# Latent attention: a tile of keys meets all 512 queries of a head in one product with the values, and the last 16 queries join the same products

## The chip, the cores and the metric

One Trainium2 chip, one of its cores. The metric is the device time of one execution of the whole program, in microseconds (us), the median of several runs. Five engines work side by side: PE (TensorE, matrix products; PEld is its loading of stationary operands), DVE (VectorE), ACT (ScalarE), POOL (GpSimd) and SP, which issues the DMAs. PE writes its results to PSUM, eight banks of 128 x 512 f32 numbers.

## What is computed

The reference is a stack of layers over 512 tokens of width 1024. Two layers of gated convolution and retention come first, then a state-space mixer with a feed-forward network, then a layer of latent attention with a second feed-forward network. Sixteen meta tokens are put ahead of the sequence for the second half, so that attention sees 528 positions. The change touches the attention alone:

```python
blocks = [(0, N_META)] + [(s, min(s + ATTN_BLOCK, L)) for s in range(N_META, L, ATTN_BLOCK)]
for s, e in blocks:
    sc = jnp.einsum('bqhd,bkhd->bhqk', q[:, s:e], k[:, :e]).astype(jnp.float32) * scale
    mask = jnp.arange(e)[None, :] <= jnp.arange(s, e)[:, None]
    p = jax.nn.softmax(jnp.where(mask, sc, -jnp.inf), axis=-1).astype(v.dtype)
    outs.append(jnp.einsum('bhqk,bkhd->bqhd', p, v[:, :e]))
```

There are 16 heads with values of width 64. The attention is causal, so a query meets only the keys up to its own position. The result needs only the 512 queries behind the meta tokens.

## The kernel before, in words

The program is written with a scheduling layer: the code names instructions and tiles, and a scheduler sets the order of the instructions on each engine, by their dependencies and the buffers that are free. A tile pool hands out buffers by tag; a tile whose tag has n buffers waits until the tile n before it has been read for the last time.

The attention runs over four groups of four heads (`b`). `project(b)` (line 1262) makes the group's keys `K`, values `v` and queries `Q` from latent rows with products of lines 382 and 397; `attend(b)` (line 1372) follows, and the scheduler mixes the projection of group b + 1 into the attention of group b. In the last group, products of the output projection (line 382, tiles `mh_a`, `ml_a`) are mixed in instead.

Inside `attend` the last 16 queries are taken first, for all four heads at once (`S`, lines 1377 to 1392): their probabilities, transposed, stand in `pt4`. Then come two pairs of heads (`hp`), and in each pair four blocks of queries (`i` = 0 to 3; 112 queries in block 0, else 128). Block i of a head meets keys 0 to 128(i + 1):

- scores: one product into a bank of three (`S`, line 1404), and one that adds the causal mask (line 1405);
- softmax (line 1353): DVE takes the maximum and scales it (1357, 1360), ACT the exponential (1363), DVE the reciprocal and the scaling (1367, 1369);
- transposes: PE turns the probabilities 128 keys at a time into one of two banks (`main2`, `main3`, line 1410), and ACT copies the bank to the tile `pT` (line 1411), of which there are three buffers;
- values: for each tile `c` of 128 keys and each head `e` of the pair one product of 64 columns of values with 112 or 128 columns of `pT` (line 1417). Head e = 0 fills partitions 0 to 63 of bank 7 (`side3`), e = 1 partitions 64 to 127.

After block 3 the last 16 queries follow, five tiles of keys for each head, products of 16 columns (line 1422). Then ACT casts the bank to `mh_a` and DVE makes the rest `ml_a` (`split`, lines 416 to 419). So a pair has 20 products of line 1417 and 10 of line 1422, and the stage has 8 pairs. An f32 product of the program shows as two instructions in the trace.

```python
for c in range(i + 1):
    for e in range(2):
        h = 2 * hp + e
        nc.tensor.matmul(op[64 * e : 64 * e + 64, q0 : q0 + M], v[:, c, 64 * h : 64 * h + 64],
                         pts[e][:, c, :M], start=(c == 0), stop=(c == i))
```

Of the kernel before, what the change touches and what calls it, by code (L numbers as in the profile page):

```python
# [9 lines left out]
F32 = mybir.dt.float32  # L10
# [7 lines left out]
P = 128  # L18
D = 1024
SEQ = 512  # L20
META = 16
T2 = SEQ + META
# [96 lines left out]
def build(ctx, tc, a):  # L119
    nc = tc.nc  # L120
# [94 lines left out]
    BANK = [PB[i // 2][:, i % 2] for i in range(4)] + side  # L215
# [195 lines left out]
    def mix_tile(name):  # L411
        h = ring.tile([P, T2], F32R, tag="mixh", name=f"mh_{name}", bufs=NRING)
        l = ring.tile([P, T2], F32R, tag="mixl", name=f"ml_{name}", bufs=NRING)
        return h, l
# [36 lines left out]
    with ExitStack() as c1:  # L451
        bp = c1.enter_context(tc.tile_pool(name="bp", bufs=1))

        def tmp(name, bufs=7):
            return bp.tile([P, 512], F32, tag="tmp", name=name, bufs=bufs)
# [164 lines left out]
        for l in range(2):  # L620

            mixc = []
            for p in range(4):
# [23 lines left out]
                for n, ps in dense((l, "z", p), X):  # L647
# [4 lines left out]
                    m = mix_tile(f"c{l}{p}{n}")  # L652
# [34 lines left out]
            for p in range(4):  # L687
# [12 lines left out]
                v = bp.tile([P, 4, 256], F32, tag="v", name=f"v{l}{p}", bufs=2)  # L700
# [14 lines left out]
                for n in range(2):  # L715
                    h = 2 * p + n
# [20 lines left out]
                    op = (D0, D1)[n]  # L737
# [12 lines left out]
                for n in range(2):  # L750
                    h = 2 * p + n
                    V.tensor_scalar(ss[:, 8 + 4 * n : 12 + 4 * n], ss[:, 8 + 4 * n : 12 + 4 * n],
                                    rc[:, 24 + h : 25 + h], None, ALU.mult)
                for n in range(2):
                    h = 2 * p + n
                    op = (D0, D1)[n]
# [8 lines left out]
                    m = mix_tile(f"r{l}{h}")  # L765
# [72 lines left out]
    with ExitStack() as c2:  # L838
# [91 lines left out]
        for g in range(8):  # L930
# [37 lines left out]
            for c, (t0, W) in enumerate(CH):  # L968
                ts_ = slice(t0, t0 + W)
                nm = f"{g}_{c}"  # L970
# [13 lines left out]
                M = sp.tile([P, 4, P], F32, tag="M", name=f"M{nm}", bufs=2)  # L984
# [12 lines left out]
                for n in range(2):  # L997
                    for cross in range(2 if c > 0 else 1):
                        for i in range(2):
                            h = 2 * n + i  # L1000
# [29 lines left out]
            if g < 7:  # L1030
# [5 lines left out]
                for i in range(4):  # L1036
                    nc.tensor.matmul(D1[32 * i : 32 * i + 32, :132], e1, sq[0][:, 132 * i : 132 * i + 132],
                                     start=True, stop=True)
# [23 lines left out]
            for n in range(2):  # L1062
                V.scalar_tensor_tensor(gz[n], gz[n], gcol(V_SNG, 2 * g + n), rb, ALU.mult, ALU.mult)
                m = mix_tile(f"s{g}{n}")
# [89 lines left out]
    with c4:  # L1154
        ap = c4.enter_context(tc.tile_pool(name="ap", bufs=1))
# [11 lines left out]
                mw[0] = ws.next(("mi", t // 2))  # L1167
            return dense2(mw[0], t % 2, X, 8)

        lsm = [tmp(f"lsm{i}", "lsm", 2) for i in range(2)]  # L1170
        lat = []
        for t in range(5):
            ps = mdense(t)
# [8 lines left out]
            else:  # L1182
                v = tmp(f"lsq{t}")
# [19 lines left out]
        def bank(kind):  # L1203
            c = cyc[kind]
            c[0] += 1
            return c[1][(c[0] - 1) % len(c[1])]
# [146 lines left out]
        def softmax(nm, S, r_, st):  # L1353

            M = S[0][0].shape[0]
            for j, (sp_, _, _) in enumerate(S):
                V.tensor_reduce(st[:M, j : j + 1], sp_, mybir.AxisListType.X, ALU.max, negate=True)
            if len(S) == 2:
                V.tensor_tensor(st[:M, 0:1], st[:M, 0:1], st[:M, 1:2], ALU.min)
            V.tensor_tensor(st[:M, 0:1], st[:M, 0:1], r_, ALU.mult)  # L1360
            p = ap.tile([P, T2], F32, tag="p", name=f"p{nm}", bufs=3)
            for j, (sp_, c0, c1_) in enumerate(S):
                nc.scalar.activation(p[:M, c0:c1_], sp_, AF.Exp, bias=st[:M, 0:1], scale=r_,
                                     accum_out=st[:M, 4 + j : 5 + j])
            if len(S) == 2:
                V.tensor_tensor(st[:M, 4:5], st[:M, 4:5], st[:M, 5:6], ALU.add)
            V.reciprocal(st[:M, 2:3], st[:M, 4:5])
            L = S[-1][2]
            V.tensor_scalar(p[:M, :L], p[:M, :L], st[:M, 2:3], None, ALU.mult)
            return p  # L1370

        def attend(b, Qh, Kh, v, rq):
            def stats(nm):
                return ap.tile([P, 8], F32, tag="st", name=f"st{nm}", bufs=4)


            S = [(bank("S")[:, :HW], HW * j, HW * j + HW) for j in range(2)]
            for j, (sp_, c0, c1_) in enumerate(S):
                for h in range(4):
                    o = sp_[32 * h : 32 * h + 32]  # L1380
                    nc.tensor.matmul(o, Qh[:, h, SEQ - 32 : SEQ], Kh[:, h, c0:c1_], start=True, stop=(j == 0))
                    if j == 1:
                        nc.tensor.matmul(o[:, HW - META :], idb[:, :32], mneg[:, META : 2 * META], start=False, stop=True)
            p = softmax(f"{b}t", S, rq[:, 16:17], stats(f"{b}t"))
            pt4 = ap.tile([P, 5, P], F32, tag="pT4", name=f"pT4{b}", bufs=1)
            pst = bank("pt")
            for c in range(4):
                nc.tensor.transpose(pst[:, P * c : P * c + P], p[:, P * c : P * c + P], ident)
            nc.scalar.copy(pt4[:, :4], pst.rearrange("p (c q) -> p c q", c=4))
            ps0 = bank("pt")[:, :P]  # L1390
            nc.tensor.transpose(ps0, p[:, T2 - P : T2], ident)
            nc.scalar.copy(pt4[:, 4], ps0)
            for hp in range(2):
                op = BANK[7]
                for i in range(4):
                    L = P * (i + 1)
                    q0 = max(0, P * i - META)
                    M = P * (i + 1) - META - q0
                    pts = []
                    for e in range(2):  # L1400
                        h = 2 * hp + e
                        nm = f"{b}{h}{i}"
                        sp_ = bank("S")[:M, :L]
                        nc.tensor.matmul(sp_, Qh[:, h, q0 : q0 + M], Kh[:, h, :L], start=True, stop=False)  # L1404
                        nc.tensor.matmul(sp_[:, L - P :], idb[:, P - M :], mneg, start=False, stop=True)
                        p = softmax(nm, [(sp_, 0, L)], rq[:M, 4 * i + h : 4 * i + h + 1], stats(nm))
                        pt = ap.tile([P, 4, P], F32, tag="pT", name=f"pT{nm}", bufs=3)
                        pst = bank("pt").rearrange("p (c q) -> p c q", c=4)
                        for c in range(i + 1):
                            nc.tensor.transpose(pst[:, c, :M], p[:M, P * c : P * c + P], ident[:M, :M])  # L1410
                        nc.scalar.copy(pt[:, : i + 1, :M], pst[:, : i + 1, :M])
                        pts.append(pt)

                    for c in range(i + 1):
                        for e in range(2):
                            h = 2 * hp + e
                            nc.tensor.matmul(op[64 * e : 64 * e + 64, q0 : q0 + M], v[:, c, 64 * h : 64 * h + 64],  # L1417
                                             pts[e][:, c, :M], start=(c == 0), stop=(c == i))
                for c in range(5):
                    for e in range(2):  # L1420
                        h = 2 * hp + e
                        nc.tensor.matmul(op[64 * e : 64 * e + 64, SEQ - META :], v[:, c, 64 * h : 64 * h + 64],
                                         pt4[:, c, 32 * h + META : 32 * h + 32], start=(c == 0), stop=(c == 4))
                m = mix_tile(f"a{b}{hp}")
                split(m, op, slice(0, SEQ))
                mix.append(m)
# [139 lines left out]
```

## Time and profile before

| | before |
|---|---|
| median of the runs (lowest to highest) | 2527.95 us (2523.36 to 2529.31), 3 runs |
| the profiled execution: its time, its span | 2524.17 us, 2522.4 us |
| instructions in the span | 41020 |
| PE, PEld, DVE, ACT, POOL busy | 98%, 87%, 64%, 43%, 6% |
| granted TensorE clock | 0.992 of full speed |
| attention stage | about 1958 to 2137 us of the span |

The profile is of one execution. Between its span and its time lie 1.8 us of start and end. Busy time of an engine is the union of its instructions; a product's shown end is a model, so two products that follow each other overlap in the rows, and the time that one really takes of PE is the distance from its start to the next one's start. "Idle before" is the time in which an engine had nothing in flight, with what ended it. Line numbers in rows are those of the kernel before.

### The profile page before, as it was taken

What the parts mean: (1) busy time and instruction counts of PE and PEld (TensorE: products, weight loads), DVE (VectorE), ACT (ScalarE), POOL (GpSimd) and SP (SyncE); (2) the same over time, 40 slices, a digit from 0 to 9 for tenths busy, and PEclk for the clock granted to TensorE, in tenths of its full rate; (3) what the DMA queues carried; (4) which work ended last, traced back from release to release, by engine and by line L of the source; (5) the groups of instructions that cost most, each with busy time, mean ns of one, the idle gap of its engine ahead of it and who ended that gap; (6) DMA issues with size and microseconds to landing.
All of it is one profiled execution on the core that took longest, in us unless ns stands there. A gap on an engine that the chain in (4) does not pass through costs nothing.

```text
span 2522.4 us, 41020 instructions
## 1 busy us (share of the span) xinstructions
PE 2460.4 (98%) x16991; PEld 2201.8 (87%) x16991; DVE 1620.4 (64%) x2968; ACT 1076.3 (43%) x2030; POOL 151.6 (6%) x177
## 2 busy tenths in 40 slices
PE   8999999989999999889999999999999999999999
PEld 7888888878888888789999998999998666999999
DVE  6743555464425554877848889777765666967764
ACT  4422332333223334455525546344344665644432
POOL 1000000100000001022202200000011000000000
PEclk9999999999999999999999999999999999999999
DMA  4333222223232222233323332233221120232322
GB/s 147 105 100 97 80 84 80 71 84 91 93 109 68 84 84 67 70 91 95 101 89 100 88 87 84 87 101 101 84 95 58 51 72 33 90 106 97 109 86 84
DMA packets 220490, 220.93 MB, mean 88 GB/s; under 512 B 8972, under 2 KB 212877, under 8 KB 220304
## 3 DMA queue, kind: packets, MB, share of 16 engines
q1 hardware_dynamic: 215648, 207.50, 26.6%
q0 software_dynamic: 4176, 10.69, 1.8%
q8 instruction: 133, 2.18, 0.3%
q14 instruction: 53, 0.43, 0.1%
q10 hardware_dynamic: 480, 0.13, 0.0%
HBM read 215.47 MB, written 2.83 MB: 87 GB/s over the span
## 4 chain that ended last, share of the span: by engine, by line
PE 84%; DVE 9%; ACT 3%; issue 2%; DMA 1%; POOL 1%; ACTq 0%; SPq 0%; DVEq 0%; POOLq 0%
PE pb L382 44%; PE main L397 7%; PE side L334 6%; PE pb L397 4%; PE main L382 3%; PE main L334 3%; PE pb L334 3%; PE pb L390 2%; PE side L1404 1%; PE side L1417 1%; DVE wlo L75 1%; PE side L1003 1%; PE side L1012 1%; PE main L1410 1%; ACT whi L74 1%
## 5 line engine op out<-in xcount | busy, mean ns | idle before, releaser
L74 ACT CAST whi<-wraw 128x1024 fp32r<-128x1024 f32 (+2 forms) x301 | 302.7, 1045 | 615.8 <-PE pb L382 430.6
L75 DVE TENSOR_TENSOR wlo<-wraw,whi 128x1024 fp32r<-128x1024 f32 (+2 forms) x301 | 364.4, 1233 | 122.5 <-ACT whi L74 120.2
L382 PE MATMUL pb<-xl_n,whi 128*128 128x264 f32 (+1 forms) x1136 | 318.1, 330 | 0.0
L382 PE MATMUL pb<-xh_n,whi 128*128 128x264 f32 (+1 forms) x1136 | 317.8, 329 | 0.3 <-DVE zu L958 0.3
L382 PE MATMUL pb<-xh_n,wlo 128*128 128x264 f32 (+1 forms) x1136 | 315.6, 329 | 0.0
L382 PEld LDWEIGHTS pb<-xh_n,whi 128*128 128x128 f32 x1136 | 192.9, 190 | 20.1 <-issue 1.2
L382 PEld LDWEIGHTS pb<-xl_n,whi 128*128 128x128 f32 x1136 | 191.9, 189 | 19.7 <-issue 1.7
L382 PEld LDWEIGHTS pb<-xh_n,wlo 128*128 128x128 f32 x1136 | 192.1, 190 | 17.6 <-issue 0.2
L382 PE MATMUL pb<-xl_l,whi 128*128 128x512 f32 x416 | 164.9, 396 | 0.0
L382 PE MATMUL pb<-xh_l,wlo 128*128 128x512 f32 x416 | 164.9, 396 | 0.0
L382 PE MATMUL pb<-xh_l,whi 128*128 128x512 f32 x416 | 164.5, 395 | 0.0
L397 PE MATMUL main<-whi,mh_w 128*128 128x256 f32 x512 | 143.8, 281 | 0.3
L397 PE MATMUL main<-whi,ml_w 128*128 128x256 f32 x512 | 143.2, 281 | 0.0
L397 PE MATMUL main<-wlo,mh_w 128*128 128x256 f32 x512 | 143.2, 281 | 0.0
L103 ACT CAST whi<-wraw 128x1024 fp32r<-128x1024 f32 x64 | 65.7, 1046 | 139.3 <-issue 54.4
L90 ACT CAST wsh<-wsr 128x512 fp32r<-128x512 f32 x96 | 58.7, 618 | 106.9 <-DVE wsr L96 62.3
L382 PE MATMUL pb<-ml_u,whi 128*128 128x264 f32 x512 | 104.2, 285 | 0.2
L382 PE MATMUL pb<-mh_u,whi 128*128 128x264 f32 x512 | 103.8, 284 | 0.0
L382 PE MATMUL pb<-mh_u,wlo 128*128 128x264 f32 x512 | 103.6, 284 | 0.0
L397 PEld LDWEIGHTS main<-whi,mh_w 128*128 128x128 f32 x512 | 96.6, 189 | 1.1 <-ACT mh_w L418 0.9
L397 PEld LDWEIGHTS main<-whi,ml_w 128*128 128x128 f32 x512 | 96.7, 189 | 0.0
L397 PEld LDWEIGHTS main<-wlo,mh_w 128*128 128x128 f32 x512 | 96.1, 188 | 0.0
(688 smaller groups left out, 6556.2 us busy)
## 6 DMA issues: line engine op xcount, KB each, us to landing
wraw<-w_in SPq DMA_DIRECT2D x63, 1024.0 KB, 5.9
wraw<-mlp_w_up SPq DMA_DIRECT2D x32, 1024.0 KB, 5.5
wraw<-mlp_w_down SPq DMA_DIRECT2D x32, 1024.0 KB, 5.3
wraw<-w_out SPq DMA_DIRECT2D x16, 1024.0 KB, 5.2
wraw<-ssd_w_in SPq DMA_DIRECT2D x16, 1024.0 KB
wraw<-ssd_w_in SPq DMA_DIRECT2D x16, 512.0 KB, 5.4
ab<-acsD POOLq DMA_DIRECT2D x32, 256.0 KB, 3.8
kR<-ke SPq DMA_DIRECT2D x32, 132.0 KB, 3.0
```

Source lines behind the costliest of these rows:

```text
L74: nc.scalar.copy(hv[s], rv[s])
L75: eng.tensor_tensor(lv[s], rv[s], hv[s].bitcast(F32), ALU.subtract)
L90: nc.scalar.copy(h, sr[:, n])
L103: nc.scalar.copy(hi[:, c], raw[:, c])
L334: nc.tensor.matmul(ps, w[wq][a][:, k], X(xq, b, k), start=(k == 0 and wq + xq == 0), stop=(k == 3 and wq == 1))
L382: nc.tensor.matmul(ps, w[wq][:, k, wsl], x(xq, k, cs), start=(k == 0 and wq + xq == 0), stop=(k == nk - 1 and wq == 1))
L390: nc.tensor.matmul(ps, w[wq][:, k, wsl], x(xq, k, cs), start=(k == 0 and wq + xq == 0), stop=(k == nk - 1 and wq == 1))
L397: nc.tensor.matmul(ps, x(xq, k, ts_), w[wq][:, k, csl], start=(k == 0 and wq + xq == 0), stop=(k == nk - 1 and xq == 1))
L1003: nc.tensor.matmul(o, xd[:W, h], M[:W, h, :W], start=True, stop=(c == 0))
L1012: nc.tensor.matmul(st[:, :256], Bt[:W], xw[:W].rearrange("p h e -> p (h e)"), start=True, stop=True)
L1404: nc.tensor.matmul(sp_, Qh[:, h, q0 : q0 + M], Kh[:, h, :L], start=True, stop=False)
L1410: nc.tensor.transpose(pst[:, c, :M], p[:M, P * c : P * c + P], ident[:M, :M])
```

## The change

For each pair of heads, `pT` becomes one tile per head, of four tiles of keys by all 512 queries. The blocks of queries are taken in the order 3, 2, 1, 0, and ACT copies each block's transposed probabilities to its columns of that tile. Beside block 3's copy one more copy takes the last 16 queries of the head out of `pt4` (first four tiles of keys) into the tile's last 16 columns. Only when all four blocks are copied come the value products: for tile `c` of keys and each head one product with all queries that see it, 512, 400, 272 and 144 columns, and one of 16 columns for the fifth tile of keys. A pair has 10 products in place of 30, with 1344 columns a head before and after. The first one is kept at its place in the program's order by `keep_in_program_order`. The tag `pT` has two buffers, four times as large, in place of three, and the two tiles `lsm` of the stage's start use one of them ahead of time.

```diff
-        lsm = [tmp(f"lsm{i}", "lsm", 2) for i in range(2)]
+        lsm = ap.tile([P, 4, SEQ], F32, tag="pT", name="lsm", bufs=2).rearrange("p c q -> p (c q)")
+        lsm = [lsm[:, T2 * i : T2 * i + T2] for i in range(2)]
...
             for hp in range(2):
-                op = BANK[7]
-                for i in range(4):
+                pts = [ap.tile([P, 4, SEQ], F32, tag="pT", name=f"pT{b}{hp}{e}", bufs=2) for e in range(2)]
+                for i in (3, 2, 1, 0):
...
-                        pt = ap.tile([P, 4, P], F32, tag="pT", name=f"pT{nm}", bufs=3)
...
-                        nc.scalar.copy(pt[:, : i + 1, :M], pst[:, : i + 1, :M])
-                        pts.append(pt)
-
-                    for c in range(i + 1):
-                        for e in range(2):
-                            h = 2 * hp + e
-                            nc.tensor.matmul(op[64 * e : 64 * e + 64, q0 : q0 + M], v[:, c, 64 * h : 64 * h + 64],
-                                             pts[e][:, c, :M], start=(c == 0), stop=(c == i))
+                        nc.scalar.copy(pts[e][:, : i + 1, q0 : q0 + M], pst[:, : i + 1, :M])
+                        if i == 3:
+                            nc.scalar.copy(pts[e][:, :, SEQ - META :], pt4[:, :4, 32 * h + META : 32 * h + 32])
+
+                op = BANK[7]
                 for c in range(5):
+                    q0 = max(0, P * c - META)
                     for e in range(2):
                         h = 2 * hp + e
-                        nc.tensor.matmul(op[64 * e : 64 * e + 64, SEQ - META :], v[:, c, 64 * h : 64 * h + 64],
-                                         pt4[:, c, 32 * h + META : 32 * h + 32], start=(c == 0), stop=(c == 4))
+                        pt = pts[e][:, c, q0:] if c < 4 else pt4[:, 4, 32 * h + META : 32 * h + 32]
+                        m = nc.tensor.matmul(op[64 * e : 64 * e + 64, q0:], v[:, c, 64 * h : 64 * h + 64], pt,
+                                             start=(c == 0), stop=(c == 4))
+                        if c + e == 0:
+                            tc.keep_in_program_order(m)
```

The scheduler builds a new order of the stage from this. In the order of PE before, the products of lines 1417 and 1422 stand in 52 groups with other work between them; here PE in group 1, first pair, block 2 (`pT102`, `pT112`: group 1, heads 0 and 1, block 2; `side3` is the bank of the values):

```order
L1404 MATMUL side2_72<-K1_17669,Q1_17668 112x128
L1405 LDWEIGHTS idb_12627
L1405 MATMUL side2_72<-mneg_12626,idb_12627 112x128
L1417 MATMUL side3_73<-pT102_18432,v1_17765 64x128
L382 MATMUL main0_17370<-ml_lat1_17115,whi154_18205 128x512
L1417 MATMUL side3_73<-pT112_18446,v1_17765 64x128
L1417 MATMUL side3_73<-pT102_18432,v1_17765 64x128
L1417 MATMUL side3_73<-pT112_18446,v1_17765 64x128
L1417 MATMUL side3_73<-pT102_18432,v1_17765 64x128
L1417 MATMUL side3_73<-pT112_18446,v1_17765 64x128
L1410 MATMUL main2_17372<-ident_79,p103_18462 128x128 x4
```

The change, PE at the end of the same pair (there the transposes are line 1409, the value products line 1420; `p110` is block 0 of head 1, `p123` block 3 of the next pair's first head):

```order
L382 MATMUL main1_17370<-mh_lat0_17060,wlo154_18157 128x512
L1409 MATMUL main3_17372<-ident_79,p110_18416 128x112
L1420 MATMUL side3_73<-pT100_18318,v1_17764 64x512
L1420 MATMUL side3_73<-pT101_18319,v1_17764 64x512
L1420 MATMUL side3_73<-pT100_18318,v1_17764 64x400
L1420 MATMUL side3_73<-pT101_18319,v1_17764 64x400
L1420 MATMUL side3_73<-pT100_18318,v1_17764 64x272
L1420 MATMUL side3_73<-pT101_18319,v1_17764 64x272
L1420 MATMUL side3_73<-pT100_18318,v1_17764 64x144
L1420 MATMUL side3_73<-pT101_18319,v1_17764 64x144
L1420 MATMUL side3_73<-pT41_18310,v1_17764 64x16 x2
L1409 MATMUL main2_17371<-ident_79,p123_18443 128x128 x4
```

All value products of the pair stand together, directly behind the last transpose of the pair. In six of the eight pairs they stand in one group so. In the first pair of group 0 and the second of group 2 the first product stands apart; PE in the first of these:

```order
L1409 MATMUL main3_17372<-ident_79,p010_17929 128x112
L1420 MATMUL side3_73<-pT000_17831,v0_17544 64x512
L1404 MATMUL side1_71<-K0_17448,Q0_17447 128x384
L1420 MATMUL side3_73<-pT001_17832,v0_17544 64x512
L1420 MATMUL side3_73<-pT000_17831,v0_17544 64x400
L1420 MATMUL side3_73<-pT001_17832,v0_17544 64x400
L1420 MATMUL side3_73<-pT000_17831,v0_17544 64x272
```

A score product of the next pair stands between head 0's first product and head 1's. On ACT, the end of group 1's first pair in the change (exponentials are line 1364, copies line 1410):

```order
L1364 ACTIVATE p110_18416,st110_18413<-side0_70,st110_18413,rq1_18136 112x128
L1410 COPY pT100_18318<-main2_17371 128x112
L1364 ACTIVATE p123_18443,st123_18440<-side1_71,st123_18440,rq1_18136 128x512
L1410 COPY pT101_18319<-main3_17372 128x112
L1364 ACTIVATE p133_18458,st133_18455<-side2_72,st133_18455,rq1_18136 128x512
L1364 ACTIVATE p122_18473,st122_18470<-side0_70,st122_18470,rq1_18136 128x384
L1322 ACTIVATE qs20_18572<-main0_17369 128x512
L418 CAST mh_a10_18432<-side3_73 128x512
L1410 COPY pT110_18436<-main2_17371 128x4x128
```

Between the last two copies that the value products wait for stands an exponential of the next pair; the cast of the bank and the next pair's first copy, which both wait for the value products, stand three instructions behind.

## Rows read from the trace of the kernel before

**Rows 1.** The chain that ended last, 1958 to 2137 us, by engine and line.

```profile
by line: PE main L382 21.0%; PE side L1404 20.1%; PE side L1417 16.0%; PE main L1410 11.0%; PE main L397 5.4%; PE side L1381 3.8%; PE side L1422 3.0%; PE main L1325 2.6%; ACT K L1274 2.6%; PE side L1405 2.4%; issue 1.8%; DVE p L1369 1.4%; A
```

**Rows 2.** Engines' busy time in the stage and in one stretch between pairs.

```profile
core 0: us, PE busy (x) PEld busy (x) DVE busy (x) ACT busy (x) POOL busy (x), PEclk, DMA share, GB/s
1958.00:2137.00 179.00, 173.21 (x1260) 118.34 (x1259) 115.31 (x417) 113.35 (x292) 7.97 (x5) 1.00 0.17 53
2004.10:2029.10 25.00, 24.71 (x202) 17.66 (x199) 15.81 (x71) 19.07 (x54) 0.00 (x0) 1.00 0.14 41
```

**Rows 3.** PE's timeline, group 1, first pair: start, length, line, out<-in, count, idle before.

```profile
2015.66 0.41 PE L1417 MATMUL side<-pT,v 128*64 128x112 f32 x2
2016.00 0.32 PE L1410 MATMUL main<-ident,p 112*128 112x112 f32 x1
...
2017.23 0.41 PE L1417 MATMUL side<-pT,v 128*64 128x112 f32 x2
2017.57 0.23 PE L1405 MATMUL side<-mneg,idb 128*128 128x128 bf16 x1
...
2019.28 1.02 PE L1404 MATMUL side<-K,Q 128*128 128x512 f32 x2
2020.23 0.66 PE L1417 MATMUL side<-pT,v 128*64 128x128 f32 x8
2020.82 0.55 PE L1410 MATMUL main<-ident,p 128*128 128x128 f32 x3
...
2022.56 0.43 PE L1417 MATMUL side<-pT,v 128*64 128x128 f32 x2
2022.92 0.50 PE L382 MATMUL main<-ml_lat,whi 128*128 128x512 f32 x1
2023.35 0.87 PE L1417 MATMUL side<-pT,v 128*64 128x128 f32 x10
2024.15 0.66 PE L1410 MATMUL main<-ident,p 128*128 128x128 f32 x4
...
2026.39 0.43 PE L1417 MATMUL side<-pT,v 128*64 128x128 f32 x2
2026.75 0.31 PE L1410 MATMUL main<-ident,p 112*128 112x112 f32 x1
...
2027.75 0.98 PE L1417 MATMUL side<-pT,v 128*64 128x128 f32 x13
...
2029.31 0.54 PE L1410 MATMUL main<-ident,p 112*128 112x112 f32 x3
```

**Rows 4.** PE's timeline, a window that holds the second of two instructions alone.

```profile
2019.71 0.59 PE L1404 MATMUL side<-K,Q 128*128 128x512 f32 x1
```

**Rows 5.** PE's timeline, the first and the last visit of the stage.

```profile
1978.83 0.41 PE L1417 MATMUL side<-pT,v 128*64 128x112 f32 x2
...
2134.79 0.98 PE L1417 MATMUL side<-pT,v 128*64 128x128 f32 x13
```

**Rows 6.** Groups of ACT in the stage by shape: count, busy us, mean ns, idle before.

```profile
L1411 ACT COPY pT<-main 128x112 f32<-128x112 f32 x16 | 3.8, 261 | 0.8 <-PE main L1410 0.7
L418 ACT CAST mh_a<-side 128x512 fp32r<-128x512 f32 x8 | 4.7, 586 | 9.1 <-PE side L1422 9.1
L1363 ACT ACTIVATE p<-side,st,rq 112x128 f32<-112x128 f32 x16 | 7.3, 457 | 0.4 <-DVE st L1360 0.4
```

**Rows 7.** ACT's timeline, the copy behind the four transposes at 2024.15.

```profile
2024.90 0.58 ACT L1411 COPY pT<-main 128x512 f32<-128x512 f32 x1 [0.68 <-PE main L1410]
```

**Rows 8.** Timeline of PE and ACT around the longest wait of a value product.

```profile
2037.05 0.40 PE L382 MATMUL main<-mh_lat,wlo 128*128 128x512 f32 x1
...
2038.48 0.47 ACT L1411 COPY pT<-main 128x384 f32<-128x384 f32 x1
...
2039.00 0.43 PE L1417 MATMUL side<-pT,v 128*64 128x128 f32 x2 [1.55 <-ACT pT L1411]
```

**Rows 9.** Waits of the stage: who waited for whom, us in total, times, longest.

```profile
PEld side L1417 <- ACT pT L1411: 10.6, 22, 2.0
```

More of the change, by code (lines that the diff above doesn't have):

```diff
@@ L1398, in attend @@
                     M = P * (i + 1) - META - q0
-                    pts = []
                     for e in range(2):
```

## The prediction

> **What bounds the kernel now.** I read the chain of waits first, for the stage that the change touches. It is nearly all PE: scores, transposes, value products (line 1417, 16.0%) and last queries (line 1422, 3.0%) stand in it beside the projections, and ACT and DVE hold a few per cent [rows 1]. The windows say the same: in the 179 us of the stage PE has something in flight for 173.2, while DVE has 115.3 and ACT 113.4, and the granted clock is 1.00, the upper level of 2.4 GHz [rows 2]. So what PE no longer has to do shortens the stage, unless ACT or DVE then fail to follow.
>
> The third view is PE's timeline over one pair of heads. Here the reader should look at distances between starts. The value products come in seven visits: 2 instructions, 2, 8, 2, 10, 2 and 34 (13 in the row, one more and the 20 of line 1422 behind it) [rows 3]. Between two score instructions of 512 columns lie 0.43 us (2019.28 to 2019.71) [rows 3, 4]; the next should start at 2020.14, and the value products start at 2020.23: **0.09 us to enter**. By the same pace an instruction of 128 columns takes 0.43 x 128 / 512 = 0.107. The eight of that visit take 0.59 until the next work starts, which fits four steps of 0.107 (two heads side by side on their halves of the array) and **0.16 to start and leave**. A visit of two instructions of one head takes 0.34 to 0.36: two steps with the other half empty, and the same overhead.
>
> **The value products before and after.** From entry to next work the seven visits take 0.34 + 0.34 + 0.59 + 0.36 + 0.80 + 0.36 + 1.56 = 4.35 us [rows 3], with 7 x 0.09 ahead of them 4.98. The order of PE has 52 visits in the stage, the first and the last at 1978.8 and 2134.8 [rows 5], 6.5 a pair, so this pair stands for the eight: 8 x 4.98 = 39.8. As a check, 19.0% of 179 us are 34.0 on the chain [rows 1], which counts the time to enter with the work before.
>
> After the change a pair is one visit. Each head streams 512 + 400 + 272 + 144 = 1328 columns in two instructions a product, both heads side by side: 2 x 1328 x 0.43 / 512 = 2.23. A step of 16 columns is what the last visit leaves: 1.56 less 0.16 less 7 x 0.107 is 0.65 for ten steps, 0.065 each [rows 3]; two remain, 0.13. With 0.09 and 0.16 that is **2.61**. The number of columns is the same; what goes is six entries and exits, the steps with one half empty, and eight of ten steps of 16 columns. Saved: 8 x (4.98 - 2.61) = 19.0.
>
> Two pairs are split: head 0's first product, 2 x 0.43 = 0.86, runs with the other half empty, and there is a further visit of 0.25. That gives back 2 x 1.1 = 2.2. **PE has 16.8 us less to do.**
>
> **What is added.** ACT gets 16 copies of 64 columns. No row has that shape; the nearest, 112 columns, takes 0.261 [rows 6]. With nothing and 0.261 as ends I take the upper: 4.2 us on ACT, hidden, since ACT would be at 117.6 of some 165 us. Uncovered they would be 4.2 us of the end.
>
> The value products now wait for the pair's last copy. From the last transpose's start this is 0.31 (the row at 2026.75), 0.09 until ACT starts (2024.15 + 0.66 to 2024.90), 0.26 of copy and 0.05 until PE starts (2038.48 + 0.47 to 2039.00), in all 0.71 [rows 3, 6, 7, 8]. The transpose's own 0.10 and the 0.09 to enter lie inside, so about 0.5 stands open where nothing lies between. By the new order three pairs are so placed (group 0's second, group 1's first, group 3's second), group 3's first has one projection product between, the others have enough. That is 1.8; ACT may also run an exponential of the next pair between the last two copies, for which I add 1.2. Today a value product's weights wait for such a copy 22 times, 10.6 in all, 0.48 each [rows 9]: eight of those would be 3.9. The ends are 0 and 8 x 1.55 = 12.4, the longest wait of today in every pair [rows 8]. I take **3**, near the mean.
>
> Behind those waiting products on PE stand the next pair's transposes; for them wait ACT's cast of the bank (0.59) and, since `pT` has two buffers, the next pair's first copy. On ACT three instructions of other work stand ahead of that cast, and on PE two sets of transposes and scores follow the products, so I cost this at nothing; without that cover it is the slower case below. The blocks' new order moves long softmaxes to the pair's start and the shortest to its end: no cost. DVE's work is the same, in another order. On SP one load of the query weights goes behind the broadcasts of a group's last head and one load of the output weights goes ahead of others; both are needed only in later work: nothing. The memory of `lsm` is free long before the first `pT`: nothing.
>
> **Sum.** 2524.17 - 16.8 + 3 = **2510.4** against the profiled execution, which stands 3.8 below the median of the runs, near their lower end. A median of new runs should lie at this or a few us above; I say 2511. With the ends of the open terms: 2504 if waits are hidden and some of today's go, 2520 if each pair waits 1.55.
>
> **The rivals.**
>
> *ACT sets the pace where the next group is projected.* In the stretch between the pairs of two groups (2004.1 to 2029.1) ACT is busy 19.07 of 25.0 us [rows 2]. With two copies more and 2.4 us less it would be 19.6 of 22.6, 87%, in a queue that runs in order. If such stretches stay as long as now, three of eight pairs give back 2.4 each: 7 us, **2517**. Against it: elsewhere in the stage ACT has a third of its time free.
>
> *PE does not bind.* In this stage weights load for only 118.3 of 179 us [rows 2], and PE waits 1.55 us for ACT at one value product [rows 8]. If the softmaxes' path through DVE and ACT sets the pace, PE's saving turns into waits: **2524**. The Trainium skill, Perfetto Trace Analysis, "Identifying the Most-Contended Engine", holds that matmul busy time is no good measure of how near PE is to its limit and that the share of weight loading is. By that rule a third of the stage would be headroom and this case likely. The distances between starts speak against it: 0.43 after 0.43 after 0.09, with no gap for a wait.
>
> *The halves do not run side by side over 512 columns.* Then a visit takes 2.3 us longer, and nothing is won: **2527** with the waits. The eight instructions in 0.59 us speak against it.
>
> *Slower: the pair becomes a closed loop.* All value products wait for the last softmax, and all copies of the next pair wait for the last value product. If the scheduler's cover is too thin, PE stands through exponential (0.46), reciprocal and scaling on DVE (taken as long), transpose, gaps and copy (0.71) before the products, and through cast and first copy (0.59 + 0.58) behind them: 2.8 [rows 6, 7]. With the exponential of the next pair in between, 3.3 a pair: 8 x 3.3 - 16.8 = 9.6 over today, **2534**. It decides from 16.8 / 8 = 2.1 of new wait a pair. For it: today's cast already waits 9.1 us in 8 times for PE [rows 6]. Against it: the order puts scores and projections of later work between.
>
> **How the numbers follow.** About 0.3%, 7.6 us, is what a measurement of this kernel can tell from no change. The forecast, 2503 to 2516, gets 0.72; ACT 0.13, half of it faster by more than 0.3%; PE not binding 0.06; halves 0.03; slower 0.06. So faster 0.77, same 0.17, slower 0.06. The range takes in the forecast's bounds and the ACT case: 2502 to 2521.
>
> **What would show it.** In the new profile the stage should be some 14 us shorter, with 10 visits of value products of about 2.6 us, each with starts of the two heads close together and steps near 0.43, 0.33, 0.23 and 0.12; the group of value products should fall from 480 instructions to 160. Waits of PE for `pT` copies should come to 3 us, not 12. ACT near 118 busy. If visits take 5 us, the halves did not overlap; if they are 2.6 and the stage is not shorter, PE's idle time will name ACT or DVE; and time that moves outside the stage would mean that the projections were only shifted.

## The result, and the profile after

| | before | after |
|---|---|---|
| median of the runs (lowest to highest) | 2526.24 us (2523.36 to 2529.31), 4 runs | 2512.99 us (2510.87 to 2515.09), 4 runs |
| the profiled execution: its time, its span | 2524.17 us, 2522.4 us | 2515.09 us, 2513.2 us |
| granted TensorE clock of that execution | 0.992 | 0.991 |

The changed kernel is faster: the ratio is 0.9947, 95% interval 0.9934 to 0.9961, which is 10 to 17 us. Forecast were 2511 us and 2502 to 2521. The two profiled executions differ by less than the medians, 9.2 us of span, since that of before lies below its median and that of after is the slowest of its four.

The windows first, with the columns of [rows 2]: the stage, which is now shorter, and the stretch from the end of group 0's last value visit to the end of group 1's first, which was 2004.28 to 2029.31 before.

```profile
core 0: us, PE busy (x) PEld busy (x) DVE busy (x) ACT busy (x) POOL busy (x), PEclk, DMA share, GB/s
1958.00:2128.50 170.50, 163.43 (x951) 107.73 (x950) 115.88 (x418) 114.71 (x310) 8.08 (x5) 1.00 0.18 55
2008.79:2031.87 23.08, 22.80 (x140) 16.18 (x139) 15.11 (x61) 18.48 (x50) 0.00 (x0) 1.00 0.17 45
```

PE's busy time falls from 173.2 to 163.4, and the stage shortens by nearly the same amount; DVE and ACT do what they did, ACT 1.4 us more. The chain that ended last, over the same stretch, answers to [rows 1]:

```profile
by line: PE main L382 20.7%; PE side L1404 18.4%; PE side L1420 13.9%; PE main L1409 10.8%; PE main L397 6.2%; PE side L1382 4.1%; PE main L1326 2.7%; ACT K L1275 2.6%; DVE p L1370 2.5%; DMA kR<-ke 2.4%; PE side L1405 1.8%; issue 1.8%; PE m
```

Lines have moved by one or three: 1420 is the value product, 1409 the transpose, 1410 ACT's copy. The value products fell from 19.0% of 179 us to 13.9% of 170.5, and more of the chain now runs through DVE (line 1370, 2.5% after 1.4%). PE's timeline shows an undivided visit:

```profile
2043.59 0.40 PE L382 MATMUL main<-mh_lat,wlo 128*128 128x512 f32 x1
2043.92 2.53 PE L1420 MATMUL side<-pT,v 128*64 128x512 f32 x20
2046.38 1.07 PE L1326 MATMUL main<-qs,sel 96*32 96x512 f32 x8
```

From its start to the next work are 2.46 us, for all twenty instructions of a pair; the visits of [rows 3] took 4.35 for the same columns.

To see where the time went, I divide the stage by PE's starts. It runs from the first product of the last queries' scores (line 1381, now 1382) to the first work behind the last value product. A visit is counted from its first start to the start of the next other work. The second kind in the table are visits of products with 32 stationary columns (lines 1381, 1383, 1325 and 1282 of before), which the change does not touch. "Rest" is what remains of the stage: other products, the time to enter visits, and waits.

| us of the profiled execution | value visits | 32-column visits | rest | stage | stage's start to span's end |
|---|---|---|---|---|---|
| before | 52: 34.4 | 11: 16.7 | 125.7 | 176.7 | 562.8 |
| after | 10: 23.7 | 18: 18.8 | 124.8 | 167.2 | 552.1 |
| change, run again (e1) | 10: 23.7 | 18: 18.8 | 124.3 | 166.7 | 551.7 |
| products in pieces (e2) | 15: 22.2 | 18: 20.7 | 125.1 | 168.0 | 552.7 |
| last queries apart (e3) | 11: 28.1 | 17: 18.4 | 122.2 | 168.8 | 555.5 |
| heads one after the other (e4) | 8: 36.0 | 18: 19.1 | 124.6 | 179.7 | 563.5 |
| blocks 0, 1, 2, 3 (e5) | 8: 25.1 | 14: 17.5 | 125.6 | 168.2 | 554.1 |
| last copies on DVE (e6) | 8: 22.1 | 18: 18.8 | 124.3 | 165.2 | 549.0 |
| before, last queries joined (e7) | 53: 32.0 | 15: 17.9 | 123.4 | 173.2 | 560.7 |
| blocks 1, 3, 2, 0 (e8) | 8: 22.1 | 18: 20.1 | 123.5 | 165.6 | 550.3 |
| second head's last copy on DVE (e9) | 8: 22.1 | 18: 18.8 | 123.8 | 164.7 | 548.5 |
| e8 and e9 together (e10) | 9: 22.8 | 18: 19.7 | 123.7 | 166.2 | 551.0 |
| two batches a pair (e11) | 26: 30.2 | 13: 16.6 | 122.2 | 169.1 | 553.7 |

The change saves 10.7 us in its own visits and pays 2.1 back in visits that it does not touch. With 0.9 from the rest that leaves 9.5 in this execution, and 10.0 in its repetition.

The stage alone is not the whole gain, because its content differs a little. The scheduler sets a different number of the output projection's products (line 382, `mh_a` and `ml_a`) into it: 36 of their instructions before, 41 after, 30 in e7, 33 in e3, 45 in e4, e6 and e9. The others follow behind the stage. One of the three groups, before and after:

```profile
L382 PE MATMUL main<-ml_a,whi 128*128 128x512 f32 x12 | 5.1, 424 | 0.0
```

```profile
L382 PE MATMUL main<-ml_a,whi 128*128 128x512 f32 x14 | 5.8, 412 | 0.0
```

From the stage's end to the span's end it is 386.1 us before (2522.4 - 2136.3) and 384.9 after (2513.2 - 2128.3), 1.2 for five instructions, 0.24 each. The last column holds both parts: there the change takes off 10.7 us, and e1 11.1.

### The profile page after: what moved, and what is told of

Read it like the earlier page. It is cut to its first block, busy times and chain, and to the rows that moved or that the text cites. A ratio compares the mean times of both kernels' runs of the same rounds, so it can differ in the third digit from the quotient of the medians.

```text
span 2513.2 us, 40393 instructions
## 1 busy us (share of the span) xinstructions
PE 2448.3 (97%) x16671; PEld 2189.0 (87%) x16671; DVE 1619.0 (64%) x2968; ACT 1077.6 (43%) x2046; POOL 151.6 (6%) x177
## 4 chain that ended last, share of the span: by engine, by line
PE 83%; DVE 9%; ACT 3%; DMA 2%; issue 2%; POOL 1%; ACTq 0%; SPq 0%; DVEq 0%; POOLq 0%
PE pb L382 44%; PE main L397 7%; PE side L334 6%; PE pb L397 4%; PE main L382 3%; PE main L334 3%; PE pb L334 3%; PE pb L390 2%; PE side L1404 1%; PE side L1420 1%; DVE wlo L75 1%; PE side L1012 1%; PE side L1003 1%; ACT whi L74 1%; PE main L1409 1%
## 5 line engine op out<-in xcount | busy, mean ns | idle before, releaser
L382 PEld LDWEIGHTS pb<-xl_n,whi 128*128 128x128 f32 x1136 | 191.6, 189 | 19.7 <-issue 1.7
```

Of the source, the lines that this page charges most:

```text
L382: nc.tensor.matmul(ps, w[wq][:, k, wsl], x(xq, k, cs), start=(k == 0 and wq + xq == 0), stop=(k == nk - 1 and wq == 1))
```

## The experiments

The kernel before was run beside each group of kernels; its medians there were 2526.48 (e1 to e4), 2526.10 (e5 to e8) and 2524.72 us (e9 to e11). A ratio's interval is about 0.0013 to either side, 3 us, so neighbours in the table are told apart by their visits and not by their medians. A profile is of one execution; that of e1 repeats both kinds of visits of the change to 0.1 us, and the rest to 0.5.

**e1: the change once more.**

> The change itself, once more, beside the other runs of this call. All theories: 0.994 to 0.996 of the time of before; ten visits of value products in the stage, 25 us together from entry to the next work.

2514.23 us, ratio 0.9958 (0.9946 to 0.9971). It is what e2 to e4 are compared with.

**e2: the same batch in 22 smaller products a pair.** A product per block of queries and tile of keys, as before, but all of a pair behind each other.

```diff
-                for c in range(5):
-                    q0 = max(0, P * c - META)
+                for i in range(4):
+                    q0 = max(0, P * i - META)
+                    q1 = P * (i + 1) - META if i < 3 else SEQ
+                    for c in range(i + 1 if i < 3 else 5):
```

> The value products stay at the end of the pair, but are cut into the blocks of queries again: 22 products a pair where the change has 10 (the last 16 queries stay joined to block 3). The order has 15 visits, seven of them of one product of 112 columns. Theory (price per visit and per column): a whole visit stays near 2.6 us and the time within 2 us of the change. Rival (price per instruction): 12 of the 20 products that were saved a pair are back, so 60% of the gain goes, about 8 us over the change.

2513.28 us, ratio 0.9950 (0.9937 to 0.9964): as the change. An undivided visit of 44 instructions takes as long as one of 20 (2073.95 to 2076.44, 2.49):

```profile
2073.95 2.56 PE L1423 MATMUL side<-pT,v 128*64 128x112 f32 x44
2076.44 0.76 PE L1409 MATMUL main<-ident,p 128*128 128x128 f32 x5
```

So the number of instructions costs nothing here; the columns and the visits do. The wide product itself, "a tile of keys meets all queries", is not what helps: that the pair's products stand together is (the last 16 queries stay joined in this run).

**e3: the last 16 queries apart again.** Ten products of 16 columns at the batch's end, and ACT's 16 extra copies left out.

```diff
-                        if i == 3:
-                            nc.scalar.copy(pts[e][:, :, SEQ - META :], pt4[:, :4, 32 * h + META : 32 * h + 32])
...
+                for c in range(5):
+                    for e in range(2):
+                        h = 2 * hp + e
+                        nc.tensor.matmul(op[64 * e : 64 * e + 64, SEQ - META :], v[:, c, 64 * h : 64 * h + 64],
+                                         pt4[:, c, 32 * h + META : 32 * h + 32], start=(c == 0), stop=(c == 4))
```

> The value products meet 496 queries at once as in the change, but the last 16 queries have their own ten products of 16 columns behind them, and the 16 small copies on ACT are gone. Theory: a visit grows by eight steps of 0.065 less 64 columns, 0.41 us, to 3.0; 3 us over the change in all. Rival (the small copies on ACT and the wait for them cost as much as the steps): the same time as the change or less.

2518.52 us, ratio 0.9970 (0.9958 to 0.9981): 4.3 above e1 in the medians, and 3.8 in the last column of the table; the visits are 4.4 longer (28.1 for 23.7). The theory had the direction but not the size: an undivided visit (2043.43 to 2046.66) grew by 0.77 and not by 0.41, and a third pair is divided. Joining the last queries pays within the batch.

**e4: head 0's five products, then head 1's.** The work is the same; only the heads no longer alternate.

```diff
-                for c in range(5):
-                    q0 = max(0, P * c - META)
-                    for e in range(2):
+                for e in range(2):
+                    for c in range(5):
+                        q0 = max(0, P * c - META)
```

> The change with the two heads' products one behind the other, five of head 0 and then five of head 1, in eight visits. Theory: two heads side by side on their halves of the array carry the visit; one behind the other a visit takes 4.8 us in place of 2.6 and the kernel 17 us more than the change, so slower than before. Rival (the halves take their instructions independently of the order in which they were written, as the starts of head 0 ahead of head 1 in the trace hint): visits stay at 2.6 and the time at that of the change.

2524.57 us, ratio 0.9994 (0.9985 to 1.0003): 10.3 above e1, and the whole gain is gone. A visit takes 4.50 us instead of 2.46:

```profile
2084.20 4.57 PE L1420 MATMUL side<-pT,v 128*64 128x512 f32 x20
2088.70 0.55 PE L1409 MATMUL main<-ident,p 128*128 128x128 f32 x3
```

So the halves of the array run side by side in the change, for 512 columns too, and they do so only if the heads alternate. That it is 10 and not 17 is no fault of this price: 8 x 4.50 is 16.3 above 8 x 2.46, but the change itself stands at 23.7 and not at 19.7, and e4 at 36.0: a difference of 12.3.

**e5: the blocks in the order 0, 1, 2, 3.** `for i in (3, 2, 1, 0)` becomes `for i in range(4)`.

> The blocks of a pair are computed in the order 0, 1, 2, 3 instead of 3, 2, 1, 0: the shortest softmax is first and the longest last. The order of PE then has eight undivided visits and no early first product. Theory (the summed length of the visits decides, and the change loses some 4.5 us there, because it divides two visits and lets the second head come late in four): eight visits of 2.55 are 20.4 us instead of 24.9, and the first pair no longer begins with its longest softmax; the last copy is longer, by 0.3 us a pair. Expected 2511, some 3 us below the change. Rival (what counts is how late the last copy of a pair is): the longest softmax and copy now stand last, and PE waits about 0.5 us more a pair: 2517 to 2518.

2517.40 us, ratio 0.9966 (0.9954 to 0.9979). The rival was right. No visit is divided, but all eight begin with one head alone, five of them for 0.74: 2113.88 to 2117.08 are 3.20 after 2.46.

```profile
2113.35 0.60 PE L1409 MATMUL main<-ident,p 128*128 128x128 f32 x4
2113.88 3.27 PE L1420 MATMUL side<-pT,v 128*64 128x512 f32 x20
2117.08 0.32 PE L1409 MATMUL main<-ident,p 112*128 112x112 f32 x1
```

Block 3's four transposes and its long copy now stand right ahead of the products. The order 3, 2, 1, 0 of the change has its use: the last copy is the shortest. The run also shows that the new order of blocks is not where the gain comes from: with the order of the kernel before, 8.7 us of it are there.

**e6: the last copy (block 0) of both heads by DVE.**

```diff
-                        nc.scalar.copy(pts[e][:, : i + 1, q0 : q0 + M], pst[:, : i + 1, :M])
+                        if i == 0:
+                            V.tensor_copy(pts[e][:, : i + 1, q0 : q0 + M], pst[:, : i + 1, :M])
+                        else:
+                            nc.scalar.copy(pts[e][:, : i + 1, q0 : q0 + M], pst[:, : i + 1, :M])
```

> The last copy of a pair (block 0, 112 columns) is made by DVE instead of ACT; eight undivided visits in the order of PE. Theory (visits are lengthened because the second head's last copy stands behind other work in ACT's queue): all visits 2.55, so 4 us below the change, 2510. Rival (DVE's queue is as late as ACT's, or the waits go elsewhere): as the change, 2514.

2512.91 us, ratio 0.9949 (0.9937 to 0.9962). Between the two: no visit is divided and the longest (3.44 in the change) is gone, but in five visits the second head still comes 0.43 late or more.

**e7: the kernel before, with the last queries joined to block 3's products.** The other half of the change alone.

> The kernel before, with only the second half of the change: the last 16 queries are copied beside block 3's and join its products; the order has 53 visits as before. By the prediction's step of 0.065 us for 16 columns: eight steps fewer, 0.52, less 0.11 for the wider products, 0.41 a pair, 3.3 us below the kernel before: 2523. By the run in which the last 16 queries had their own products again (0.77 us longer for an undivided visit, 4.3 us in all): 4 to 6 us below it, 2520 to 2522. If the value products' waits and entries are all that counts, no difference: 2526.5.

2523.35 us, ratio 0.9990 (0.9981 to 0.9999): 2.75 below before, where the prediction's step of 0.065 us gives 3.3. A pair's last visit falls from 1.56 (2080.91 to 2082.47 in the kernel before) to 1.20:

```profile
2083.75 1.07 PE L1420 MATMUL side<-pT,v 128*64 128x144 f32 x13
...
2084.78 0.24 PE L1424 MATMUL side<-pT,v 128*64 128x16 f32 x2
2084.95 0.32 PE L1410 MATMUL main<-ident,p 112*128 112x112 f32 x1
```

The stage is 3.5 shorter, but six instructions of the output projection have gone behind it; in the last column the gain is 2.1. So of the change's 13 us some 2 to 3 belong to the last queries. The batch alone, e3, has 8.0.

**e8: the blocks in the order 1, 3, 2, 0.**

> The blocks of a pair in the order 1, 3, 2, 0: a short softmax first, the longest second, the shortest last; eight undivided visits in the order of PE. Theory (summed length of visits, and the late last copy matters little): 2.55 each, 4 us below the change, 2510, and the fastest of these. Rival (the order of the softmaxes costs nothing, and the waits are where PE's cover is thin whatever the order): as the change, 2514.

2512.09 us, ratio 0.9947 (0.9934 to 0.9959): between the two. The visits of 2.55 each did not come: they take 2.46 to 2.94. In all the value visits are 1.6 us shorter, the 32-column visits 1.3 longer.

**e9: only the second head's last copy by DVE,** so that the two last copies run on two engines (e6's edit with `if i == 0 and e == 1`).

> The change, but the last copy of the second head (block 0, 112 columns) is made by DVE, that of the first head stays on ACT, so the two last copies run beside each other; eight undivided visits in the order of PE. Theory (the second head comes late because the two last copies stand one behind the other on one engine, 0.40 to 0.44 us in most pairs with both on one engine): visits of 2.55, 20.5 in all instead of 23.1 with both on DVE, 2510 to 2511. Rival (the second head's transpose is late anyway, or DVE comes to it late): visits as with both on DVE, 2513.

2512.10 us, ratio 0.9949 (0.9933 to 0.9964). My theory fell: the visits are to 0.01 us those of e6. The timeline (start, length, engine, line) shows why:

```profile
2022.40 0.26 PE L1409 MATMUL main<-ident,p 112*128 112x112 f32 x1
...
2022.59 1.08 PE L1423 MATMUL side<-pT,v 128*64 128x512 f32 x3
2022.70 0.27 DVE L1411 COPY pT<-main 128x112 f32<-128x112 f32 x1
...
2023.03 0.19 PEld L1423 LDWEIGHTS side<-pT,v 128*64 128x64 f32 x3 [0.25 <-DVE pT L1411]
```

The second head's last transpose starts at 2022.40, its copy at 2022.70 (the reduction ahead of it on DVE, 0.55 from 2022.01, is over by then), and the head's first weights at 2023.03, while head 0 has gone ahead at 2022.59. What is late is the second head's own chain of transpose, copy and weights, 0.63 us, not a queue on one engine. Only other work of PE between the last transpose and the products hides it, as at 2043.92 in the change.

**e10: the order 1, 3, 2, 0 with e9's copy.**

> Order 1, 3, 2, 0 of the blocks, and the second head's last copy on DVE; nine visits, one divided. Theory (the lengths of the visits add up): 7 x 2.55 and a divided one of 3.7, 21.5 us, 1.6 below the order 1, 3, 2, 0 alone: 2510.5, the fastest of all if the two remedies add up. Rival (what is saved inside a visit comes back as a wait outside it): 2512, as the order alone.

2515.18 us, ratio 0.9965 (0.9952 to 0.9978). The two remedies do not add up: one visit is divided again, five come late by 0.43, and the stage is 166.2. Its runs are 9.5 us below before, the last column of its profile 11.8; the 2 us between them are within the interval.

**e11: two batches a pair,** blocks 3 and 2 with the last queries, then blocks 1 and 0.

```diff
+                    if i % 2:
+                        continue
+                    op = BANK[7]
+                    a, z, n = (240, SEQ, 5) if i else (0, 240, 2)
+                    for c in range(n):
+                        q0 = max(a, P * c - META)
```

> The pair's products in two batches: blocks 3 and 2 with the last 16 queries (272, 272, 272, 144 and 16 columns) as soon as these are copied, then blocks 1 and 0 (240 and 128 columns); the order has 26 visits, nine batches divided. The columns are the same. Theory (the summed length of the visits decides; what the change gave back outside them is not the size of the batch): sixteen batches of 1.6 and 1.2, 8 x 2.8, and nine divisions at 0.7 are 29 us, 4 above the change: 2517 to 2519. Rival (the whole pair's batch holds up transposes, copies and softmaxes behind it, and that costs the 5 us that the change lost outside its visits): half of it comes back, 2513 to 2515.

2516.78 us, ratio 0.9967 (0.9956 to 0.9978): above e1 by 2.3 us in the ratios and by 4.3 against the medians of before, with 2.4 more in the stage than e1. Both were partly right. The 26 visits cost 6.5 us more than the change's ten, more than I had worked out, but in this profile the 32-column visits are back at 16.6, 2.2 less, and the rest is 2.6 lower although it holds 16 more entries of 0.09. So most of the 6.5 comes back outside the value visits. Of what the rest gives back, 2.8 us show as waits: PE has nothing in flight for 4.3 us of this stage, for 7.1 in the change.

None of these kernels beats the change by more than its interval; e2, e6, e8 and e9 are level with it.

## Why the prediction was right, and where it was not

**Visits.** Ten were forecast, ten came. An undivided one should have taken 2.52 (2.61 less 0.09 of entry) and took 2.46. The two divided ones were costed at 0.86 + 0.16 = 1.02 for head 0 alone, and took 1.01 from 1991.26 to 1992.27:

```profile
1991.05 0.29 PE L1409 MATMUL main<-ident,p 112*128 112x112 f32 x1
1991.26 1.07 PE L1420 MATMUL side<-pT,v 128*64 128x512 f32 x2
1992.27 0.91 PE L1404 MATMUL side<-K,Q 128*128 128x384 f32 x2
```

By these terms the visits should have fallen from 34.8 to 8 x 2.52 + 2 x 1.02 = 22.2. They fell from 34.4 to 23.7. What is over is the next term's.

**Waits, the step that was mis-sized.** I took 3 us for the waits on a pair's last copy. New waits of 4.4 us came, and of two kinds, of which I had only the first. About 2 us, those on the copies, are inside the visits: 2005.35 to 2008.79 is 3.44, 0.98 over 2.46; 2028.84 to 2031.87 is 0.57 over, 2125.47 to 2128.34 is 0.41 over. The first one, in PE's timeline, then ACT's, then the weight loads':

```profile
2005.15 0.26 PE L1409 MATMUL main<-ident,p 112*128 112x112 f32 x1
2005.35 3.51 PE L1420 MATMUL side<-pT,v 128*64 128x512 f32 x20
2008.79 0.39 PE L382 MATMUL main<-mh_lat,whi 128*128 128x264 f32 x1
```

```profile
2004.63 0.40 ACT L1276 ACTIVATE ks<-main 128x264 f32<-128x264 f32 x1
2005.04 0.97 ACT L1275 ACTIVATE K<-main,gc 64x264 f32<-64x264 f32 x2
2006.03 0.25 ACT L1410 COPY pT<-main 128x112 f32<-128x112 f32 x1
```

```profile
2005.34 0.19 PEld L1420 LDWEIGHTS side<-pT,v 128*64 128x64 f32 x2 [0.41 <-issue]
2006.34 0.20 PEld L1420 LDWEIGHTS side<-pT,v 128*64 128x64 f32 x4 [0.80 <-ACT pT L1410]
```

Three instructions of the next group's projection stand ahead of the copy in ACT's queue; head 1 starts at 2006.34, 0.99 behind head 0. This is the rival "ACT sets the pace" on a small scale.

The other part is outside the visits. The rest should have fallen by 42 entries of 0.09, 3.8, and by the wait of 1.55 in [rows 8], and grown by 1.2 for the products that moved into the stage; it fell by 0.9, so 3.2 us are left over. Most of that can be seen as idle time: PE has nothing in flight for 5.8 us of the stage before (179.0 - 173.2) and for 7.1 after (170.5 - 163.4). Of the old idle time 1.7 stood ahead of value products and is gone, and 0.6 of the new lies in the 32-column visits, so the rest has 2.4 us of new idle time. The other 0.8 no view shows as a wait; seven more entries into 32-column visits would be 0.6 of it, if one of those costs 0.09 too. The waits of the stage name some of the new ones:

```profile
ACT mh_a L418 <- PE side L1420: 8.7, 5, 3.8
...
PEld main L1409 <- DVE p L1370: 5.8, 10, 1.7
...
PEld side L1420 <- ACT pT L1410: 2.6, 6, 0.8
```

The value products' own waits went from 10.6 [rows 9] to 2.6, and ACT's cast waits 8.7 after 9.1 [rows 6], as costed. But the transposes now wait for softmaxes: their weights for 5.8 us after 1.9 in the kernel before, and PE's idle time ahead of them was 1.1, is 3.2 now (2.5 in e1), and 1.5 with two batches. The groups of PE, of before, after and e11:

```profile
L1410 PE MATMUL main<-ident,p 128*128 128x128 f32 (+1 forms) x160 | 28.2, 281 | 1.1 <-DVE p L1369 1.1
```

```profile
L1409 PE MATMUL main<-ident,p 128*128 128x128 f32 (+1 forms) x160 | 27.2, 278 | 3.2 <-DVE p L1370 2.4 <-DVE st L1368 0.5 <-ACT K L1275 0.4
```

```profile
L1409 PE MATMUL main<-ident,p 128*128 128x128 f32 (+1 forms) x160 | 28.1, 279 | 1.5 <-DVE p L1370 1.1
```

My reading, which no run tests by itself, is that small value visits had filled these gaps, which a batch cannot. The longest new wait is in the pair of group 1 that held the stall of [rows 8]: PE waits 1.25 for a softmax.

```profile
2038.63 0.39 PE L382 MATMUL main<-ml_lat,whi 128*128 128x512 f32 x1
2040.27 0.77 PE L1409 MATMUL main<-ident,p 128*128 128x128 f32 x5 [1.25 <-DVE p L1370]
```

**What the prediction did not have at all: the 32-column visits,** 11 in 16.7 us before, 18 in 18.8 after. In the kernel before two groups of such products ran side by side in one visit of 2.80 us, 0.29 of it a wait:

```profile
2005.57 1.08 PE L1381 MATMUL side<-K,Q 128*32 128x264 f32 x10
2006.42 0.64 PE L1282 MATMUL main<-ks,sel 128*32 128x264 f32 x5
...
2007.81 0.63 PE L1282 MATMUL main<-ks,sel 128*32 128x264 f32 x2 [0.29 <-ACT ks L1275]
2008.37 0.39 PE L397 MATMUL main<-whi,mh_lat 128*128 128x256 f32 x1
```

After, the scores of the same group are cut in three by transposes, 0.56 + 1.16 + 1.44 us with 0.87 of waits at their ends, and the sums of line 1283 come later by themselves:

```profile
2000.29 0.63 PE L1382 MATMUL side<-K,Q 128*32 128x264 f32 x2
2000.85 0.44 PE L1409 MATMUL main<-ident,p 128*128 128x128 f32 x2
2001.22 0.64 PE L1382 MATMUL side<-K,Q 128*32 128x264 f32 x4
2002.38 0.41 PE L1409 MATMUL main<-ident,p 128*128 128x128 f32 x2 [0.52 <-DVE st L1368]
2002.72 0.85 PE L1382 MATMUL side<-K,Q 128*32 128x264 f32 x9
...
2004.16 0.29 PE L1409 MATMUL main<-ident,p 112*128 112x112 f32 x1 [0.35 <-ACT K L1275]
```

Two instructions that stand alone take 0.56, where six take 0.57:

```profile
2087.99 0.65 PE L1382 MATMUL side<-K,Q 128*32 128x264 f32 x6
2088.56 0.32 PE L1409 MATMUL main<-ident,p 112*128 112x112 f32 x1
```

The heads' products run beside each other, and a cut group pays its pass again. I had read the new order for value products alone. That the batch is what cuts them is only weakly borne out (11 and 15 such visits without a batch of a pair, 13 with two batches, 14 to 18 with one), and no run undid the cutting alone.

**Costs that were right.** The 16 copies of 64 columns take 4.1 us, and ACT has 114.7 busy (forecast 118):

```profile
L1412 ACT COPY pT<-pT 128x64 f32<-128x64 f32 x16 | 4.1, 256 | 3.0 <-PE side L1420 2.9
```

The joined steps of 16 columns were 3.3 us by the prediction and 2.75 in e7; inside the batch (e3) they are worth more, 3.8 to 4.3.

**The sum.** Forecast: 16.8 saved, 3 given back, 13.8. The stage and what follows it show 10.7 and, in e1, 11.1; the medians differ by 13.3 and 12.3, each known to some 3 us. So the gain is between 10 and 13. By the trace the visits and entries save 16.5 (34.4 - 23.7, with the 2.0 of waits that the visits now hold, and 42 x 0.09), where 16.8 were forecast. Against them stand 4.4 of new waits (2.0 in the visits, 2.4 outside), less the 1.7 of old ones that are gone and that the sum had left in, and 2.1 of cut visits. That leaves 11.7, about 1 us more than the trace shows; the entries into seven more 32-column visits may be 0.6 of it. So the 3 for waits is near the net 2.7, but partly by luck: the new waits were under-sized, and old ones went. What the sum lacks is a term for the cut visits.

The forecast of 2511 lies 2 to 3 us too low. About 2 us of that are its base, since the profiled execution on which the sum stands is 2 us quicker than the median of before, and 0.6 was added for it. By the medians the 13.8 is then 0.5 to 1.5 too large, by the trace 3; the spread of the runs does not tell which is nearer.

**The rivals.** That the halves do not run side by side fell with e4. That ACT sets the pace fell too: such stretches did not stay as long as they were. The one between groups 0 and 1 took 23.1 us after 25.0, with ACT busy for 18.5 of them (the windows of the result), and the other two, counted in the same way from visit's end to visit's end, took 31.6 after 36.9 and 20.7 after 25.2. That PE does not bind fell with the windows: 9.8 us less of PE's work, 9.5 less of stage. The Trainium skill, Perfetto Trace Analysis, "Identifying the Most-Contended Engine", would judge by the share of weight loading, and beside it by the share of peak arithmetic, which the prediction left out and no run here works out. The share of weight loading was 66% before and is 63% after (107.7 of 170.5), and the time followed PE's products, so by that share alone the rule misleads here. The slower closed loop did not come: new waits are about 0.55 us a pair (4.4 / 8) and not the 2.1 from which it decides.

What stays open: which softmax or copy causes which of the 2.4 us outside the visits, and why the 32-column groups are cut. A third buffer of `pT` was not tried, nor the kernel before with the new order of blocks alone.

## What to carry to other kernels

Count how often PE enters a group of products that use a part of the array, not how many instructions the group has: here 44 instructions in one visit cost as much as 20, and seven visits, some with one half empty, took 1.9 us more than one. Let products on the two halves alternate, and put some other product between the last transpose and a batch that needs its copy, or one half runs alone for 0.4 us. When an order is made by a scheduler, count the visits of all groups before and after, those that the change does not touch too; a large batch may also take away small pieces that used to fill waits elsewhere (my reading of the 2.4 us above).

## What the runs showed of the hardware that I had not expected

The two halves are not held together by the order of the program. In the visit at 2005.35 head 1 is 0.99 late, and from then on each head runs at its own pace. The groups by shape in the 0.07 us from 2007.95 on:

```profile
L1420 PE MATMUL side<-pT,v 128*64 128x400 f32 x1 | 0.5, 499 | 0.0
L1420 PE MATMUL side<-pT,v 128*64 128x272 f32 x1 | 0.4, 393 | 0.0
L1420 PE MATMUL side<-pT,v 128*64 128x16 f32 x2 | 0.3, 220 | 0.0
```

Head 0 is at its last products, of 16 columns, while head 1 begins its 272; in the program head 1's 272 and 144 stand ahead of head 0's 16. The Trainium skill, TensorE: Matmul & The Clock Gate, "The mechanism", says that products start and end in program order; this trace shows otherwise for products on different columns of the array. How far one half may run ahead has a limit: with all of head 0's products first (e4) the visit is 4.50 us, and head 1's first product starts at 2086.24, 2.05 us behind head 0's, when head 0 is at its products of 144 columns.
